# Padding tiles in SBUF so that a matmul's two operands start at chosen offsets, with a one-tile first load and a reordered tail, in a hybrid retention and SSD layer

## The chip, the cores and the metric

The kernel runs on one core of a Trainium2 chip. The core has a matrix engine (PE, with a queue PEld for weight loads), a vector engine (DVE), an activation engine (ACT), a general engine (POOL) and a queue that issues DMAs (SP). Each takes its instructions in order. Time is device microseconds of one execution, the median of three runs.

## What is computed

One layer over 16 learned meta tokens and 512 frames (L = 528) with a model width of 1024, all in float32:

```python
hn = _rmsnorm(h, norm1_w[i])
proj = (hn @ w_in[i]) * valid[None, :, None]
q, k, v, g, z, xbc, dt_raw = _split_cols(proj)
y_ret = _retention(q, k, v, g, pos, ret_norm_w[i])
y_ssd = _ssd(z, xbc, dt_raw, valid, conv_w[i], conv_b[i], dt_bias[i], a_log[i],
             d_skip[i], ssd_norm_w[i])
h = h + jnp.concatenate([y_ret, y_ssd], axis=-1) @ w_out[i]
u = _rmsnorm(h, norm2_w[i]) @ w_ff1[i]
h = h + jnp.square(jax.nn.relu(u)) @ w_ff2[i]
return _rmsnorm(h, final_norm_w)[:, CHUNK:]
```

`_retention` has 8 heads with decay over chunks of 64 frames and rotary q and k. `_ssd` (Mamba-2) has 4 groups of 4 heads: `x`, `B` and `C` go through a causal convolution of width 4 and silu, the step size `dt` through softplus, the chunks through a scan, and the result is gated by silu(z) and normalised.

## The kernel before, in words

Every large product is done with three matmuls on the fast float32 form: each operand is split into a high part (ACT, line 164) and a low part (DVE, line 165, source minus high part), and high x high, high x low and low x high are summed in PSUM (lines 342 to 344, `mm_k`). The normalised input stands transposed in SBUF as `hnh` and `hnl`, [128, 8 K tiles, 576] each, of which 528 columns are used. In `mm_cols` the weights (`wh`, two halves for high and low) are the stationary operand and a piece of the 528 columns is the moving one; 528 is more than the 512 columns of a PSUM bank, so each output tile is made in two pieces, `HV` = 272 and 256 columns, with 8 x 3 = 24 matmuls each. `C` leaves the first 12 columns out and has 260 and 256. In the `z` products (line 473) the columns of `hnh` and `hnl` are the stationary operand and the 256 weight columns move. FF1 (line 998) multiplies quarters of the weights with quarters `hs1` to `hs7` of the activations, 256 columns at a time (a Strassen-like scheme with 7 products); `wo` and FF2 have 512 columns and aren't touched.

Where in SBUF a tile starts follows from the pools: each tile is placed behind the last. `wh_tile` moves the start of a weight tile by 16 floats (64 bytes) per class `cls`, for which each tile is 128 floats longer than it needs to be:

```python
t = pool.tile([P, 8 * ZN], F32R, tag="w", name="wh")
return t[:, 16 * cls:16 * cls + 2048].rearrange("p (y n) -> p y n", y=2)
```

In time order the program has: the start (0 to 20 us: loads of the first weights `wzr` by ACT's queue and of the transposed input `xf` by SP's, `NWARM` matmuls on zeros that PE does meanwhile, the splits of both, the first `z` product), four SSD groups (20 to 187 us), eight retention heads (187 to 412), the output product (to 500), FF1 (to 672), FF2 with the tail (to 845).

An SSD group makes `B`, `C` and two `x` tiles: matmuls to a PSUM tile `pj`, DVE's eviction to `pre` (line 407), convolution in four DVE steps into `acc` (423, 425), silu on ACT into `bf`, `cf` or `xf` (427; this `xf` is not the input of the start). PE transposes those (`mtp`, `btp`, `xtp`), and ACT and DVE copy them out (`btm`, `bt`, `xmw`, `xdw`). In the first group PE sums the decays (`acs`, `acst`); ACT takes exponentials (`tea`, `cd`), which needs another activation table than silu, loaded by an ACT_TABLE_LOAD. `acst` goes through DRAM (`acsd`) and comes back as four broadcasts `lt`, to which DVE adds (509) and of which ACT takes the exponential (510). `zs` is silu(z) from PSUM (474), `mixs` copies the group's result (611).

The order in which the code is written isn't the order on the engines: the tile framework's scheduler orders instructions of each engine by its own estimates, inside what dependencies allow, except for instructions marked with `keep_in_program_order`.

At the end `fin_b(b)` adds the last half of token block b (1065, DVE), squares it (1067, ACT), `scale_b` of the block before follows (1083 on DVE, 1085 on ACT, with a DMA each), and POOL makes the block's 1/rms `rss`; the last block is done in two pieces of 256 columns.

Of the kernel before, what the change touches and what calls it, by code (L numbers as in the profile page):

```python
# [19 lines left out]
LP = 576  # L20
NWARM = 10
LAG = 2
# [53 lines left out]
def kernel(ctx, tc, x, meta, xtr, wzd, nfw, w_in, w_out, w1, w2, hrows, pcols, crope, cmask, cpack, cident, out, gpow):  # L76
# [66 lines left out]

    warm(NWARM)
    HV = ((0, 272), (272, 256))

# [3 lines left out]
    mt = startp.tile([M, D], F32, name="mt")  # L150
    for k in range(0, KT, 2):
        nc.scalar.dma_start(out=wzr[:, k:k + 2], in_=wzd[:, k:k + 2])
    for t0, n in HV:
        for k in range(0, KT, 2):
            o = KT + KT * t0 + k * n
            e = o + 2 * n
            if o == KT:
                o = 0
            nc.sync.dma_start(out=xf[:, o:e], in_=xtr[:, o:e])
# [46 lines left out]

    def u_z(w, c0, cls):

        loads = [(lambda r: r.rearrange("p (k c) -> p k c", c=256),
                  w[:, c0:c0 + 256].rearrange("(k p) c -> p k c", p=P))]  # L210
        return Unit(loads, lambda r, j: r[:, j * 1024:(j + 1) * 1024].rearrange("p (k c) -> p k c", c=256), 256, (cls, cls))

    class UnitZ0(Unit):
# [7 lines left out]

        def pair(self, k):

            j, k0 = divmod(k, 4)
            if k0 == 0:
                t = whl.tile([P, 8 * ZN], F32R, tag="w", name="wz").rearrange("p (y k c) -> p y k c", y=2, c=ZN)
                self.parts[j] = (t[:, 0], t[:, 1])
            hv, lv = self.parts[j]
            split(hv[:, k0:k0 + 2], lv[:, k0:k0 + 2], wzr[:, k:k + 2])

# [14 lines left out]
    for g in range(SG):  # L245
        add(("bc", g), u_cols(w_in, C_B + P * g, C_C + P * g))
        add(("x", g), u_cols(w_in, C_X + 256 * g, C_X + 256 * g + P, (1, 1)))
        if g:
            add(("z", g), u_z(w_in, C_Z + 256 * g, (g - 1) % 3))
    for h in range(RH):  # L250
        add(("qk", h), u_cols(w_in, C_Q + P * h, C_K + P * h, (1, 2)))
        add(("vg", h), u_cols(w_in, C_V + P * h, C_G + P * h, (3, 1)))
    for hf in range(2):
# [71 lines left out]
    nc.sync.dma_start(out=cst, in_=cpack)  # L325
    for k in range(0, KT, 2):
        if k:
            order[0].pair(k)
        for kk in (k, k + 1):
            gain_split(0, kk, ACT if k else DVE)  # L330
        if not k:
            order[0].pair(k)
    st["prep"] = 2
# [66 lines left out]
    def conv_silu(key, j, ct, tag, bufs, res, name, t_in=0, t_out=0, hook=None):  # L400
        wh, wl = part(key, j)
        pre = sw.tile([P, 3 + L], F32, tag="pre", name="pre")
        if t_in == 0:
            DVE.memset(pre[:, 0:3], 0.0)

        def evict(ps, t0, n):
            DVE.tensor_tensor(pre[:, 3 + t0:3 + t0 + n], ps[:, :n], rsr[:, t0:t0 + n], op=ALU.mult)

        out = []
        for t0, n in ((t_in, 272 - t_in), (272, 256)):  # L410
            ps = psum(pp, "pj")
            mm_cols(ps, n, wh, wl, t0)
            out.append((ps, t0, n))
            if not hook:
                evict(*out.pop())
        if hook:
            hook()
            for o in out:
                evict(*o)
        acc = sw.tile([P, L], F32, tag="acc", name="acc", bufs=1)  # L420
        cw = PC_CW + 4 * ct
        ts = slice(t_out, L)
        DVE.tensor_scalar(acc[:, ts], pre[:, t_out:L], pc[:, cw:cw + 1], None, op0=ALU.mult)
# [232 lines left out]
    def ret_proj(h, r):  # L656
# [10 lines left out]
        wh, wl = part(("qk", h), 1)  # L667
        for t0, n in HV:
            ps = psum(pp, "pk")
            mm_cols(ps, n, wh, wl, t0)  # L670
            rope_piece(kr, kt, ps, t0, n, t0)
# [3 lines left out]
        wh, wl = part(("vg", h), 0)  # L675
        for t0, n in HV:
            ps = psum(pp, "pv")
            mm_cols(ps, n, wh, wl, t0)
            ACT.activation(vf[:, t0:t0 + n], ps[:, :n], AF.Copy)
# [172 lines left out]

    def split_hs(q, pool, src):
        t = HS.get(q)
        if t is None:
            t = HS[q] = pool.tile([P, 2, 4, 256], F32R, name=f"hs{q}")
        split(t[:, 0].rearrange("p k n -> p (k n)"), t[:, 1].rearrange("p k n -> p (k n)"), src)

    def tok_gen(b):
# [4 lines left out]
        for j in range(2):  # L864
# [6 lines left out]
            if b == 1:  # L871
                split_hs(1 + j, None, R[j][0])
            yield
# [6 lines left out]
        while "t" not in FP:  # L880
            yield
        split_hs(6, FP["t"], t2)
        yield
        split_hs(5, FP["t"], R[0][0])
        sub(R[0][1], R[1][1], R[0][1])
        yield
        split_hs(7, FP["t"], R[0][1])
        yield
        sub(R[1][0], R[1][0], t2)
        split_hs(4, FP["t"], R[1][0])  # L890
        yield
        split_hs(3, FP["t"], R[1][1])

# [49 lines left out]
    def w1_prep(n, pool=None):  # L943
        if n >= len(seq) or n in wsp:
# [3 lines left out]
               5: lambda: s1s[g], 6: lambda: quarter(g, 0, 0), 7: lambda: quarter(g, 1, 0)}[q]()  # L948
        t = wh_tile(pool or whl, 1)
        split(t[:, 0, :], t[:, 1, :], src)  # L950
# [127 lines left out]
    def scale_b(b):  # L1078
        o = out[b * P:(b + 1) * P, :]
        w = 256 if b == NB - 1 else 512  # L1080
        for c in range(0, 512, w):
            l, r = slice(c, c + w), slice(512 + c, 512 + c + w)
            DVE.scalar_tensor_tensor(yo[b][:, r], xt[b][:, r], rss[b], nwb[:, r], op0=ALU.mult, op1=ALU.mult)
            nc.sync.dma_start(out=o[:, r], in_=yo[b][:, r])
            ACT.activation(yo[b][:, l], yo[b][:, l], AF.Copy, scale=rss[b])
            nc.scalar.dma_start(out=o[:, l], in_=yo[b][:, l])
# [66 lines left out]
```

## Time and profile before

| | us |
|---|---|
| median of 3 runs | 845.76 |
| lowest, highest | 845.34, 850.91 |
| profiled execution, of which span | 847.17, 845.4 |
| PE busy | 832.1 |
| DVE busy | 556.5 |
| ACT busy | 411.2 |

The profile is one execution; its span runs from the first to the last instruction, and 1.8 us lie around it. Busy time counts an engine's instructions, and matmuls overlap each other: a matmul of 256 columns is listed with 0.28 us although the next one starts after less than half of that. PE's granted clock was 0.998 of full speed in the mean.

### The profile page before, as it was taken

What the parts mean: (1) busy time and instruction counts of PE and PEld (TensorE: products, weight loads), DVE (VectorE), ACT (ScalarE), POOL (GpSimd) and SP (SyncE); (2) the same over time, 40 slices, a digit from 0 to 9 for tenths busy, and PEclk for the clock granted to TensorE, in tenths of its full rate; (3) what the DMA queues carried; (4) which work ended last, traced back from release to release, by engine and by line L of the source; (5) the groups of instructions that cost most, each with busy time, mean ns of one, the idle gap of its engine ahead of it and who ended that gap; (6) DMA issues with size and microseconds to landing.
All of it is one profiled execution on the core that took longest, in us unless ns stands there. A gap on an engine that the chain in (4) does not pass through costs nothing.

```text
span 845.4 us, 13366 instructions
## 1 busy us (share of the span) xinstructions
PE 832.1 (98%) x5556; PEld 759.2 (90%) x5556; DVE 556.5 (66%) x874; ACT 411.2 (49%) x693; POOL 29.8 (4%) x62
## 2 busy tenths in 40 slices
PE   8999999999999999999999999999999999999996
PEld 7999999999889999999888889999999888888884
DVE  6788997968745554556365539988887554474442
ACT  7755737272422233232453548577667643354432
POOL 1000000010000000000000000000000000010001
PEclk9999999999999999999999999999999999999999
DMA  9751333332331313131213213333334523332002
GB/s 316 252 178 50 100 101 100 95 106 76 101 100 50 100 51 100 51 101 50 100 53 102 96 50 100 101 100 101 100 101 137 188 100 99 100 100 100 0 1 100
DMA packets 85373, 84.70 MB, mean 100 GB/s; under 512 B 2464, under 2 KB 67744, under 8 KB 85312
## 3 DMA queue, kind: packets, MB, share of 16 engines
q1 hardware_dynamic: 84016, 81.68, 30.7%
q10 hardware_dynamic: 1296, 2.16, 0.7%
q8 instruction: 43, 0.70, 0.3%
q14 instruction: 18, 0.15, 0.1%
HBM read 81.71 MB, written 2.13 MB: 99 GB/s over the span
## 4 chain that ended last, share of the span: by engine, by line
PE 90%; DVE 3%; ACT 3%; DMA 2%; issue 2%; POOL 0%; POOLq 0%; ACTq 0%; SPq 0%
PE acc L781 10%; PE acc L782 10%; PE acc L780 10%; PE fb L998 7%; PE fd L998 5%; PE fa L998 4%; PE pz L473 3%; PE pj L344 3%; PE pj L342 3%; PE pj L343 3%; PE pv L344 2%; PE pv L343 2%; PE pv L342 2%; PE pk L342 2%; PE pk L344 2%; PE pk L343 2%
## 5 line engine op out<-in xcount | busy, mean ns | idle before, releaser
L164 ACT ACTIVATE wh<-wr 128x1024 fp32r<-128x1024 f32 x146 | 153.8, 1057 | 207.2 <-issue 81.6
L165 DVE TENSOR_TENSOR wh<-wr,wh 128x1024 fp32r<-128x1024 f32 x146 | 177.8, 1219 | 107.4 <-ACT wh L164 107.2
L781 PE MATMUL acc<-wh,mh 128*128 128x512 f32 x370 | 144.1, 390 | 0.5 <-DVE mh L165 0.5
L780 PE MATMUL acc<-wh,mh 128*128 128x512 f32 x370 | 144.2, 391 | 0.0
L782 PE MATMUL acc<-wh,mh 128*128 128x512 f32 x370 | 144.1, 389 | 0.0
L781 PEld LDWEIGHTS acc<-wh,mh 128*128 128x128 f32 x370 | 69.5, 188 | 15.0 <-DVE mh L165 0.9
L782 PEld LDWEIGHTS acc<-wh,mh 128*128 128x128 f32 x370 | 69.5, 188 | 14.6
L780 PEld LDWEIGHTS acc<-wh,mh 128*128 128x128 f32 x370 | 69.4, 188 | 14.0
L342 PE MATMUL pj<-hnh,wh 128*128 128x256 f32 (+2 forms) x256 | 73.7, 288 | 0.0
L343 PE MATMUL pj<-hnl,wh 128*128 128x256 f32 (+2 forms) x256 | 73.2, 286 | 0.0
L344 PE MATMUL pj<-hnh,wh 128*128 128x256 f32 (+2 forms) x256 | 72.5, 283 | 0.0
L998 PE MATMUL fb<-hs,wh 128*128 128x256 f32 x576 | 68.4, 277 | 0.4 <-DVE wh L165 0.4
L998 PEld LDWEIGHTS fb<-hs,wh 128*128 128x128 f32 x576 | 66.8, 188 | 0.7 <-DVE wh L165 0.6
L343 PEld LDWEIGHTS pj<-hnl,wh 128*128 128x128 f32 x256 | 48.5, 189 | 0.1
L342 PEld LDWEIGHTS pj<-hnh,wh 128*128 128x128 f32 x256 | 48.4, 189 | 0.0
L344 PEld LDWEIGHTS pj<-hnh,wh 128*128 128x128 f32 x256 | 48.4, 189 | 0.0
L998 PE MATMUL fa<-hs,wh 128*128 128x256 f32 x384 | 46.3, 277 | 0.3 <-ACT a_lo L1003 0.3
L998 PE MATMUL fd<-hs,wh 128*128 128x256 f32 x384 | 45.2, 277 | 0.0
L998 PEld LDWEIGHTS fa<-hs,wh 128*128 128x128 f32 x384 | 44.7, 188 | 0.5 <-ACT a_lo L1003 0.5
L998 PEld LDWEIGHTS fd<-hs,wh 128*128 128x128 f32 x384 | 44.5, 188 | 0.1
L164 ACT ACTIVATE mh<-a_lo 128x512 fp32r<-128x512 f32 x48 | 29.3, 621 | 19.2 <-PE acc L782 17.1
L165 DVE TENSOR_TENSOR mh<-a_lo,mh 128x512 fp32r<-128x512 f32 x48 | 32.5, 687 | 7.7 <-ACT mh L164 7.6
(270 smaller groups left out, 1646.6 us busy)
## 6 DMA issues: line engine op xcount, KB each, us to landing
wr<-in_w_ff_dram SPq DMA_DIRECT2D x30, 1024.0 KB, 5.3
wr<-in_w_in_dram SPq DMA_DIRECT2D x40, 512.0 KB, 4.8
wr<-in_w_out_dram SPq DMA_DIRECT2D x8, 1024.0 KB, 5.0
wr<-in_w_in_dram SPq DMA_DIRECT2D x7, 1024.0 KB, 8.1
lt<-acsd SPq DMA_DIRECT2D x16, 256.0 KB, 4.2
xt<-in_x_dram SPq DMA_DIRECT2D x4, 512.0 KB, 6.8
a_lo<-in_w_ff_dram SPq DMA_DIRECT2D x2, 1024.0 KB, 6.4
wzr<-in_wzd_dram ACTq DMA_DIRECT2D x4, 272.0 KB, 6.1
```

What stands on the lines that cost most here:

```text
L164: ACT.activation(dst_h, src, AF.Copy)
L165: DVE.tensor_tensor(dst_l, src, dst_h.bitcast(F32), op=ALU.subtract)
L342: PE.matmul(ps[:, :n], lhsT=wh[:, k, :], rhs=hnh[:, k, t0:t0 + n], start=(k == 0), stop=False)
L343: PE.matmul(ps[:, :n], lhsT=wh[:, k, :], rhs=hnl[:, k, t0:t0 + n], start=False, stop=False)
L344: PE.matmul(ps[:, :n], lhsT=wl[:, k, :], rhs=hnh[:, k, t0:t0 + n], start=False, stop=(k == KT - 1))
L473: PE.matmul(o, lhsT=a[:, k, tk], rhs=zp[k // 4][y][:, k % 4, :], start=(i == 0), stop=(i == len(seq) - 1))
L780: PE.matmul(acc[b], lhsT=s[:, 0, tk], rhs=wh[:, kk, :], start=(k == 0), stop=False)
L781: PE.matmul(acc[b], lhsT=s[:, 1, tk], rhs=wh[:, kk, :], start=False, stop=False)
L782: PE.matmul(acc[b], lhsT=s[:, 0, tk], rhs=wl[:, kk, :], start=False, stop=(k == nk - 1))
L998: PE.matmul(o, lhsT=w[:, y, k, cs], rhs=h[:, z, k, :], start=(q in (1, 6, 5) and t == 0 and k == 0 and i == 0), stop=(k == 3 and i == 2), ...
```

## The change

`hnh`, `hnl` and the `hs` tiles get pads of 64 bytes ahead (and of 192 behind), so that they start 64 bytes past a multiple of 256; all weight tiles that are stationary start at class 2 (128 bytes), and the moving weights of `z` at class 1 (64 bytes). The pieces of 528 columns are cut 256 and 272, in this order, where they were 272 and 256, so that the second piece starts at a multiple of 256 bytes behind the first; `C` has 244 and 272. With that the 256- and 272-column products have (moving, stationary) start at (64, 128) modulo 256 bytes, `z` of the first group aside. `hs3` to `hs7` are now allocated together. The first two loads of `wzr` and `xf` hold one K tile each, and their splits are done likewise; `NWARM` goes from 10 to 8. In `scale_b` the two scalings keep their place in program order, which puts the last block's sum ahead of the scaling of the block before.

```diff
-NWARM = 10
+NWARM = 8
...
+    hnp.tile([P, 16], F32, name="pad7")
     hnh, hnl = [hnp.tile([P, KT, LP], F32R, name=n)[:, :, :L] for n in ("hnh", "hnl")]
+    hnp.tile([P, 48], F32, name="pad8")
...
-    HV = ((0, 272), (272, 256))
+
+    HV, PV = ((0, 272), (272, 256)), ((0, 256), (256, 272))
...
-    for k in range(0, KT, 2):
-        nc.scalar.dma_start(out=wzr[:, k:k + 2], in_=wzd[:, k:k + 2])
+    KP = ((0, 1), (1, 2), (2, 4), (4, 6), (6, 8))
+    for k, e in KP:
+        nc.scalar.dma_start(out=wzr[:, k:e], in_=wzd[:, k:e])
     for t0, n in HV:
-        for k in range(0, KT, 2):
+        for k, e in KP if t0 == 0 else ((0, 2),) + KP[2:]:
             o = KT + KT * t0 + k * n
-            e = o + 2 * n
+            e = o + (e - k) * n
...
-        return Unit(loads, lambda r, j: r[:, j * 1024:(j + 1) * 1024].rearrange("p (k c) -> p k c", c=256), 256, (cls, cls))
+        return Unit(loads, lambda r, j: r[:, j * 1024:(j + 1) * 1024].rearrange("p (k c) -> p k c", c=256), 256, (1, 1))
...
-        add(("x", g), u_cols(w_in, C_X + 256 * g, C_X + 256 * g + P, (1, 1)))
+        add(("x", g), u_cols(w_in, C_X + 256 * g, C_X + 256 * g + P))
         if g:
-            add(("z", g), u_z(w_in, C_Z + 256 * g, (g - 1) % 3))
+            add(("z", g), u_z(w_in, C_Z + 256 * g))
     for h in range(RH):
-        add(("qk", h), u_cols(w_in, C_Q + P * h, C_K + P * h, (1, 2)))
-        add(("vg", h), u_cols(w_in, C_V + P * h, C_G + P * h, (3, 1)))
+        add(("qk", h), u_cols(w_in, C_Q + P * h, C_K + P * h))
+        add(("vg", h), u_cols(w_in, C_V + P * h, C_G + P * h))
...
-        for t0, n in ((t_in, 272 - t_in), (272, 256)):
+        for t0, n in ((t_in, 256 - t_in), (256, 272)):
...
-        for t0, n in HV:
+        for t0, n in PV:
             ps = psum(pp, "pk")
...
+    hs12.tile([P, 16], F32, name="pad3")
     HS = {q: hs12.tile([P, 2, 4, 256], F32R, name=f"hs{q}") for q in (1, 2)}
+    hs12.tile([P, 48], F32, name="pad4")
...
-        t = wh_tile(pool or whl, 1)
+        t = wh_tile(pool or whl, 2)
...
-            DVE.scalar_tensor_tensor(yo[b][:, r], xt[b][:, r], rss[b], nwb[:, r], op0=ALU.mult, op1=ALU.mult)
+            tc.keep_in_program_order(
+                DVE.scalar_tensor_tensor(yo[b][:, r], xt[b][:, r], rss[b], nwb[:, r], op0=ALU.mult, op1=ALU.mult))
             nc.sync.dma_start(out=o[:, r], in_=yo[b][:, r])
-            ACT.activation(yo[b][:, l], yo[b][:, l], AF.Copy, scale=rss[b])
+            tc.keep_in_program_order(ACT.activation(yo[b][:, l], yo[b][:, l], AF.Copy, scale=rss[b]))
             nc.scalar.dma_start(out=o[:, l], in_=yo[b][:, l])
```

The lines of the file move by 4 to 9. The scheduler orders the SSD groups otherwise, too, on all engines. Three places of it follow; `x3` behind a row is a count, and numbers behind a name tell buffers apart.

ACT in the first SSD group before, from the convolutions of `C` and the first `x` tile on:

```order
L164 ACTIVATE wh<-wr 128x1024
L427 ACTIVATE cf<-acc,pc 128x512
L378 ACTIVATE acst<-acs 16x512
L427 ACTIVATE xf<-acc,pc 128x528
L392 ACT_TABLE_LOAD
L392 ACTIVATE tea<-tna 128x80
L391 ACTIVATE dt_436<-dt_436 128x80
L393 ACTIVATE cd<-acst 128x80
L527 ACTIVATE bt<-btp 128x384
```

and after:

```order
L168 ACTIVATE wh<-wr 128x1024
L432 ACTIVATE cf<-acc,pc 128x512
L168 ACTIVATE wh<-wr 128x1024
L383 ACTIVATE acst<-acs 16x512
L397 ACT_TABLE_LOAD
L397 ACTIVATE tea<-tna 128x80
L432 ACT_TABLE_LOAD
L432 ACTIVATE xf<-acc,pc 128x528
L396 ACT_TABLE_LOAD
L396 ACTIVATE dt_440<-dt_440 128x80
L398 ACTIVATE cd<-acst 128x80
L532 ACTIVATE bt<-btp 128x384
```

`xf` of the first `x` tile stood between `acst` and the table load of the exponentials; now a split is ahead of `acst`, `tea` with its table load is ahead of `xf`, and silu's table is loaded again.

DVE in the first SSD group before, around the second `x` tile (`pre` of 256 columns is its first row):

```order
L407 TENSOR_TENSOR pre<-pj,rsr 128x256
L423 TENSOR_SCALAR acc<-pre,pc 128x528
L425 SCALAR_TENSOR_TENSOR acc<-pre,pc,acc 128x528
L165 TENSOR_TENSOR wh<-wr,wh 128x1024
L425 SCALAR_TENSOR_TENSOR acc<-pre,pc,acc 128x528
L407 TENSOR_TENSOR pre<-pj,rsr 128x272
L425 SCALAR_TENSOR_TENSOR acc<-pre,pc,acc 128x528
L509 TENSOR_SCALAR lt<-lt,tna 128x128 x5
L407 TENSOR_TENSOR pre<-pj,rsr 128x256
L509 TENSOR_SCALAR lt<-lt,tna 128x128 x5
```

and after:

```order
L412 TENSOR_TENSOR pre<-pj,rsr 128x256
L514 TENSOR_SCALAR lt<-lt,tna 128x128 x3
L412 TENSOR_TENSOR pre<-pj,rsr 128x272
L514 TENSOR_SCALAR lt<-lt,tna 128x128
L428 TENSOR_SCALAR acc<-pre,pc 128x528
L399 TENSOR_TENSOR tdw<-tdt,dt_440 128x80
L430 SCALAR_TENSOR_TENSOR acc<-pre,pc,acc 128x528
L514 TENSOR_SCALAR lt<-lt,tna 128x128
L430 SCALAR_TENSOR_TENSOR acc<-pre,pc,acc 128x528
L514 TENSOR_SCALAR lt<-lt,tna 128x128
L430 SCALAR_TENSOR_TENSOR acc<-pre,pc,acc 128x528
L514 TENSOR_SCALAR lt<-lt,tna 128x128
```

The additions to `lt`, which wait for its DMA, stood behind the tile's convolution and now stand ahead of the eviction of its second piece and between the steps.

ACT in the second SSD group before, around the silu of its second `x` tile (`xf`) and of the first three of its four `z` pieces (`zs`):

```order
L474 ACTIVATE zs<-pz,rsc 128x256
L427 ACTIVATE xf<-acc,pc 128x528
L474 ACTIVATE zs<-pz,rsc 128x256
L510 ACT_TABLE_LOAD
L510 ACTIVATE lt<-lt 128x512
L474 ACT_TABLE_LOAD
L474 ACTIVATE zs<-pz,rsc 128x256
L523 ACTIVATE btm<-mtp 16x128
```

and after:

```order
L479 ACTIVATE zs<-pz,rsc 128x256
L616 ACTIVATE mixs<-ytp,pc 128x512
L432 ACTIVATE xf<-acc,pc 128x528
L515 ACT_TABLE_LOAD
L515 ACTIVATE lt<-lt 128x512
L479 ACT_TABLE_LOAD
L479 ACTIVATE zs<-pz,rsc 128x256
L616 ACTIVATE mixs<-ytp,pc 128x512
L479 ACTIVATE zs<-pz,rsc 128x256
```

Before, two `zs` follow each other with one `xf` between; now the second `zs` stands behind `xf`, a load, `lt` and another load, and half of the `mixs` copies stands behind it.

## Rows read from the trace of the kernel before

**Rows 1.** The page's part 1, and the weight splits' subtractions on DVE (part 5).

```profile
PE 832.1 (98%) x5556; PEld 759.2 (90%) x5556; DVE 556.5 (66%) x874; ACT 411.2 (49%) x693; POOL 29.8 (4%) x62
...
L165 DVE TENSOR_TENSOR wh<-wr,wh 128x1024 fp32r<-128x1024 f32 x146 | 177.8, 1219 | 107.4 <-ACT wh L164 107.2
```

**Rows 2.** Whom PE waited for: line, releaser, us in total, times, longest.

```profile
PE st L553 <- ACT btm L523: 0.7, 1, 0.7
```

**Rows 3.** Timeline of PE: start, us, instruction; first and last counted row of pieces.

```profile
38.55 0.29 PE L342 MATMUL pj<-hnh,wh 128*128 128x272 f32 x1
...
41.40 0.29 PE L344 MATMUL pj<-hnh,wh 128*128 128x272 f32 x1
...
43.90 0.28 PE L343 MATMUL pj<-hnl,wh 128*128 128x256 f32 x1
...
46.53 0.28 PE L344 MATMUL pj<-hnh,wh 128*128 128x256 f32 x1
...
253.00 0.29 PE L344 MATMUL pk<-hnh,wh 128*128 128x272 f32 x1
...
255.66 0.29 PE L344 MATMUL pk<-hnh,wh 128*128 128x272 f32 x1
255.79 0.28 PE L342 MATMUL pk<-hnh,wh 128*128 128x256 f32 x1
...
258.39 0.28 PE L344 MATMUL pk<-hnh,wh 128*128 128x256 f32 x1
...
561.28 2.09 PE L998 MATMUL fa<-hs,wh 128*128 128x256 f32 x17
```

**Rows 4.** Timeline of ACT at the start.

```profile
2.92 1.28 ACT L164 ACT_TABLE_LOAD   x1 [2.92 <-issue]
5.35 0.66 ACT L164 ACTIVATE wz<-wzr 128x544 fp32r<-128x544 f32 x1 [1.15 <-DMA wzr<-in_wzd_dram]
```

**Rows 5.** Timeline of PE and DVE at the end.

```profile
835.73 1.52 PE L807 MATMUL acc<-wh,mh 128*128 128x512 f32 x6
...
837.87 0.75 DVE L1083 SCALAR_TENSOR_TENSOR yo<-xt,rss,nwb 128x512 f32<-128x512 f32 x1 [1.69 <-POOL rss L1074]
838.54 0.87 DVE L1065 SCALAR_TENSOR_TENSOR xt<-acc,rs,xt 128x256 f32<-128x256 f32 x2
```

**Rows 6.** Timeline of ACT, DVE and PE in the first SSD group.

```profile
38.80 1.06 ACT L164 ACTIVATE wh<-wr 128x1024 fp32r<-128x1024 f32 x1 [2.77 <-issue]
39.08 0.74 DVE L425 SCALAR_TENSOR_TENSOR acc<-pre,pc,acc 128x512 f32<-128x512 f32 x1
...
39.89 0.43 DVE L407 TENSOR_TENSOR pre<-pj,rsr 128x272 f32<-128x272 f32 x1
40.24 0.23 DVE L368 SCALAR_TENSOR_TENSOR dtv<-dtv,dt 128x80 f32<-128x80 f32 x1
...
42.73 0.59 ACT L378 ACTIVATE acst<-acs 16x512 f32<-16x512 f32 x1 [2.15 <-PE acs L377]
...
44.80 0.74 ACT L427 ACTIVATE xf<-acc,pc 128x528 f32<-128x528 f32 x1 [1.48 <-DVE acc L425]
...
45.55 1.28 ACT L392 ACT_TABLE_LOAD   x1
...
46.65 0.27 PE L519 MATMUL mtp<-idt,xf 128*16 128x128 f32 x1
```

**Rows 7.** Timeline of DVE, first addition to `lt`.

```profile
53.87 1.07 DVE L509 TENSOR_SCALAR lt<-lt,tna 128x128 f32<-128x128 f32 x5 [1.81 <-DMA lt<-acsd]
```

**Rows 8.** Tile `lt`: time from issue to landing of its DMAs.

```profile
DMA to landing us min/median/max: 3.2/4.2/7.4
```

**Rows 9.** Timeline of ACT and PE's weight loads in the fourth SSD group.

```profile
178.51 0.74 ACT L427 ACTIVATE xf<-acc,pc 128x528 f32<-128x528 f32 x1 [1.69 <-DVE acc L425]
...
182.51 0.47 ACT L474 ACTIVATE zs<-pz,rsc 128x256 f32<-128x256 f32 x1
...
183.98 0.19 PEld L473 LDWEIGHTS pz<-wh,hnh 128*128 128x128 f32 x1 [0.22 <-ACT zs L474]
```

More of the change, by code (lines that the diff above doesn't have):

```diff
@@ L205, in u_cols, with u_z @@
         return Unit(loads, views, P, cls)
-    def u_z(w, c0, cls):
+    def u_z(w, c0):
         loads = [(lambda r: r.rearrange("p (k c) -> p k c", c=256),
                   w[:, c0:c0 + 256].rearrange("(k p) c -> p k c", p=P))]
-        return Unit(loads, lambda r, j: r[:, j * 1024:(j + 1) * 1024].rearrange("p (k c) -> p k c", c=256), 256, (cls, cls))
+        return Unit(loads, lambda r, j: r[:, j * 1024:(j + 1) * 1024].rearrange("p (k c) -> p k c", c=256), 256, (1, 1))
     class UnitZ0(Unit):
@@ L220, in load, with tiles @@
             pass
-        def pair(self, k):
+        def tiles(self, k, e):
             j, k0 = divmod(k, 4)
@@ L228, in pair @@
             hv, lv = self.parts[j]
-            split(hv[:, k0:k0 + 2], lv[:, k0:k0 + 2], wzr[:, k:k + 2])
+            e0 = k0 + e - k
+            split(hv[:, k0:e0], lv[:, k0:e0], wzr[:, k:e])
     def u_rows(w, k0, c0):
@@ L325 @@
     nc.sync.dma_start(out=cst, in_=cpack)
[L326 to L332, printed above, removed]
+    for k, e in KP:
+        if k > 1:
+            order[0].tiles(k, e)
+        for kk in range(k, e):
+            gain_split(0, kk, ACT if k > 1 else DVE)
+        if k < 2:
+            order[0].tiles(k, e)
     st["prep"] = 2
@@ L675, in ret_proj @@
         wh, wl = part(("vg", h), 0)
-        for t0, n in HV:
+        for t0, n in PV:
             ps = psum(pp, "pv")
@@ L851, with split_hs @@
     FP = {}
[L853 to L856, printed above, removed]
+    def split_hs(q, src):
+        t = HS[q]
         split(t[:, 0].rearrange("p k n -> p (k n)"), t[:, 1].rearrange("p k n -> p (k n)"), src)
@@ L871, in tok_gen @@
             if b == 1:
-                split_hs(1 + j, None, R[j][0])
+                split_hs(1 + j, R[j][0])
             yield
@@ L881, in tok_gen @@
             yield
-        split_hs(6, FP["t"], t2)
+        split_hs(6, t2)
         yield
-        split_hs(5, FP["t"], R[0][0])
+        split_hs(5, R[0][0])
         sub(R[0][1], R[1][1], R[0][1])
         yield
-        split_hs(7, FP["t"], R[0][1])
+        split_hs(7, R[0][1])
         yield
         sub(R[1][0], R[1][0], t2)
-        split_hs(4, FP["t"], R[1][0])
+        split_hs(4, R[1][0])
         yield
-        split_hs(3, FP["t"], R[1][1])
+        split_hs(3, R[1][1])
     def fin1(b, acc):
@@ L1039, in first_products @@
                 FP["t"] = tc.alloc_tile_pool(name="hst", bufs=1, side="right", reuse_waits="tile")
+                FP["t"].tile([P, 16], F32, name="pad5")
+                HS.update({q: FP["t"].tile([P, 2, 4, 256], F32R, name=f"hs{q}") for q in (6, 5, 7, 4, 3)})
+                FP["t"].tile([P, 48], F32, name="pad6")
             if n == at[(6, 0)]:
```

## The prediction

> **What bounds the kernel now.** I read the page first. PE is busy 98% of the span, DVE 66%, ACT 49% [rows 1]; so time is won by matmuls that follow each other faster, by a shorter start or end, or by removing the few waits of PE. Next I read what PE waits for: the longest single wait after the start is 0.7 us, for ACT's copy of `btm` in the first SSD group [rows 2]. There is thus little to win from waits and much room to lose: an engine that is off the chain today needs to fall behind by a microsecond only once to show in the end. Third, I read the start-to-start time of matmuls of one size at different places of the program, since a matmul's listed length (0.28 us) overlaps the next one.
>
> **Part 1, the addresses.** In the built program the tiles start at multiples of 64 bytes; I write (moving, stationary) for the two operands' first bytes modulo 256. The pitch is the start of a later row minus that of an earlier one, divided by the number of matmuls between [rows 3]:
> 256 columns at (64,128), retention `pk`: (258.39 - 255.79)/23 = 113.0 ns. 256 columns at (64,64), the second `x` tile: (46.53 - 43.90)/22 = 119.5 ns. 256 columns at (0,64), FF1: (2.09 - 0.28)/16 = 113.1 ns. 272 columns at (0,128), `pk`: (255.66 - 253.00)/21 = 126.7 ns. 272 columns at (0,64), `x`: (41.40 - 38.55)/23 = 123.9 ns.
> What is quick in these rows is the stationary operand 64 bytes past the moving one, (0,64) and (64,128); a difference of 0 or 128 costs 5 to 6% at 256 columns and 2% at 272. The change puts all of these at (64,128). For 256 columns that case has its row, 113.0. For 272 it has none: between 113.0 x 272/256 = 120.1 (if only the columns counted) and 126.7 (no better than now); I take 123.9, the row with the same difference.
> The sum: `x`, 192 matmuls of 256 columns from 119.5 to 113.0, 1.25 us; `pv`, 192 of 256 columns at (64,192), priced like `x`, 1.25; `z` of groups 1 to 3, of whose 288 matmuls two thirds have a difference that isn't 64, another 192 x 6.5 ns = 1.25; 272 columns of `pk`, `pv` and `B`, 480 x 2.8 ns = 1.34. `x`'s own 272-column pieces gain nothing (123.9 already), `C` has 516 columns in two pieces before and after, the 1344 matmuls of FF1 run at 113 already, and the 512-column products keep their difference. Total **-5.1 us**. The ends come from the 768 pieces of 272 columns: 3.8 ns less each gives -8.0, 2.8 ns more gives -2.9.
> The Trainium skill's page "TensorE: Matmul & The Clock Gate", section "Back-to-back issue gap", gives N/2.4 + 2.5 ns for a single stream, whatever the operands' addresses: an estimate of 109 ns at 256 columns and 116 at 272. The trace lies 4 to 11 ns above it and differs by address, so it doesn't bear this out; if the rule held, this part would be worth nothing (the third rival).
>
> **Part 2, the start.** ACT issues five pieces of `wzr` in place of four. In the built program the fifth issue waits for the landing of the first piece, because eight DMA semaphores are used in turn, and behind it on ACT's queue stand the table load and the first weight split. Before, the load ran at 2.92 to 4.20, beside the transfer, and the split at 5.35 when `wzr` had landed [rows 4]. Now a piece of half the size may land some 0.6 us earlier (half of the 1.15 that ACT waited after the load), the load (1.28) follows it, and the first split starts near 6.0 (5.9 to 6.6) instead of 5.35. The pieces behind it land when they did before. So of this at most 0.5 to 1.3 us reach PE, and most of it is caught up, because PE waits for the second pair's landing anyway. Fewer warm matmuls end PE's warm stretch two matmuls earlier. I take **+0.4 us**, ends -0.1 (the smaller first piece wins after all) and +1.4 (nothing is caught up).
>
> **Part 3, the end.** PE's last matmul ends at 837.25. DVE then first waits for POOL's `rss` of block 2, scales it at 837.87, and starts the last block's sum at 838.54 [rows 5]. In the new order the sum stands first and can start about 837.4, so 1.1 us earlier; behind it come ACT's squares, POOL, the last scale and the output DMAs. Block 2's scale then falls into POOL's time; its own DMA issue (0.37 us on ACT) may hold the last scale by 0.1. **-1.0 us**, ends -0.7 and -1.2.
>
> **Part 4, what the reorder moves along.** With the pieces of `x`, `B`, `C` swapped, the scheduler writes other orders on ACT, DVE and SP all through the SSD groups. No row of before shows these orders; I bound each place from the rows of the work that now stands in the queue.
> First group, ACT: `xf` of the first `x` tile stood ahead of a table load and now stands behind two, one for `tea`'s exp and one back to silu; a third follows it. DVE, which finished the convolution of `C` at 39.82 before, now has in front of that: a weight split's subtraction (1.2), an eviction (0.35 to the next start) and four short steps (0.15 each by the same count), 2.1 us in all, so it is done near 41.9 [rows 1, 6]. From there ACT does `cf` and `xf`, 0.74 each, a split 1.06, `acst` 0.59, two loads of 1.28 and the small `tea`, some 0.2: 5.9 us, less some 0.1 of overlap at each of four places: 47.4. PE stood at the transposes of that tile at 46.65 without a wait; the same matmuls are ahead of them now and save about 0.3. Wait **+1.1** (0 to 2.7).
> Second place in that group: DVE's additions to `lt`, which waited 1.81 us for the broadcast DMA [rows 7] at a point where little depended on them, now stand in front of the eviction and the convolution of the second `x` tile. The DMA needs 3.2 to 7.4 us to land after its issue [rows 8]; with 3.2, since no weight load stands ahead of it any more, the convolution (some 3.7 us with the `lt` steps between) ends 0.5 to 1 us after PE needs it, and `btm`, for which PE waited 0.7, comes behind more `lt` steps: **+1.5** (0 to 3.0).
> Second group: ACT now has, after the second `x` tile's `xf`: load, `lt`, load, `zs`, half of `mixs`, `zs`. The `z` pieces use PSUM banks that only `zs` frees, so PE's fourth piece stands behind that queue. The fourth group has this very order before already: from `xf` at 178.51 to `zs` at 182.51 it took 4.0 us, and PE waited only 0.22 for it [rows 9], because it had a `z` piece of 24 matmuls (2.7 to 2.9 us by the pitches above) and eleven transposes to do. In the new order seven of those eleven stand ahead of the fourth piece, an estimated 0.1 us less for each that is gone: a wait of 0.6 if `xf` ends with PE's piece. In the second group DVE's convolution stands behind `lt` as well, which may hold `xf` by up to 2.4: 3.0 in all. **+1.3** over before, nearer to the fourth group's row. Groups three and four, without that delay: **+0.4** each (0 to 1.2).
> Total 1.1 + 1.5 + 1.3 + 0.8 = **+4.7 us**, ends 0 and +11.
> The Trainium skill's "ScalarE: Activation LUTs", section "What ACT_TABLE_LOAD costs", puts a set switch at 2.66 us, 1.28 load and 1.38 drain. The trace shows no drain: the fourth group's 4.0 us [rows 9] hold `xf` 0.74, two loads of 1.28 and `lt`, some 0.6. By that section's figure the first place alone would be an estimated 2.8 us worse.
>
> **Sum.** -5.1 + 0.4 - 1.0 + 4.7 = -1.0 us on the profiled execution's 847.17 (span 845.4). That run lies 1.4 above the median of 845.76; taken from the median, the forecast is **844.8 us**.
>
> **Rivals.**
> (a) The new orders cost nothing: DVE and ACT are 66% and 49% busy [rows 1], and before's longest wait stays below 0.7 us, and in the fourth group the same order of ACT costs 0.22 [rows 2, 9]. Against it: at the first two places PE has no slack. Then -5.1 + 0.4 - 1.0 = -5.7: 840.1, with 272 columns at 120.1 ns 837.2.
> (b) Slower: ACT's order around `zs` is paid in full in each of the groups two to four. If the fourth `z` piece waits 3.0 us in each, with 2.6 from the first group, the waits sum to 11.6, and the kernel takes 845.76 + 11.6 - 5.1 + 0.4 - 1.0 = 851.7. It decides where DVE's convolution ends more than about 1 us after PE's second `z` piece in all three groups. For it: `xf` in the fourth group waited 1.69 us for DVE already [rows 9]. Against: the fourth group's row, 0.22.
> (c) The pitch doesn't follow the addresses, but what runs beside the matmuls; then the change doesn't do what it says, and 0.4 - 1.0 + 4.7 = +4.1 remains: 849.9. Against it: the pitches are constant over whole pieces of 24 matmuls, in stretches with quite different work on the other engines.
>
> **Chances.** Forecast 0.55, (a) 0.27, (b) 0.12, (c) 0.06. The range that leaves out 2 in 10 goes from 838.5 (most of (a)) to 852.5 ((b)'s value with most of the start's bound). A measurement of this kernel tells about 1% from no change, 8.5 us: below 837.3 only with (a) and 120.1 ns together, 0.07; above 854.2 only with (b) and the late start, 0.06; the rest, 0.87.
>
> **What would show it.** Part 1: the pitch of `pv`'s and `x`'s 256-column pieces falls to 113 ns, and that of the 272-column pieces says which bound held. Part 2: the first weight split at 5.9 to 6.6. Part 3: the last block's sum right behind PE's end. Part 4: waits of PE on ACT's `xf`, `btm` and `zs` near 42 to 100 us, of 1 to 3 us each. The prediction is wrong if those waits stay below 1 us in all (then (a)), or if the products of the retention heads, whose order hardly changes, don't get faster (then (c)).

## The result and the profile after

The changed kernel takes 856.13 us in the median of 20 runs (850.20 to 858.48), before 848.33 in as many (845.29 to 851.63). The ratio is 1.0081, with a 95% interval of 1.006 to 1.0102: slower by about 7 us. The forecast was 844.8, the range 838.5 to 852.5. Both kernels have executions that are about 5 us longer than their others (of before's 20, ten took 845.3 to 846.3 us and ten 850.3 to 851.6), from a stretch of FF1 that the last section shows, so that a median also depends on how many of them there were; the two profiles compared here have none of it (847.17 before, 852.28 after).

The page of the changed kernel:

```profile
span 850.5 us, 13363 instructions
PE 832.0 (98%) x5554; PEld 759.7 (89%) x5554; DVE 557.9 (66%) x875; ACT 408.1 (48%) x692; POOL 28.3 (3%) x62
```

PE's busy time is the same as in [rows 1], but the span is 5.1 us longer. By the first matmuls of each stage, PE is 0.8 us late at the first `pj` (20.76, before 19.94), 7.7 at the first `pq` of the heads (194.78, before 187.06), 5.6 at the output product (417.66, before 412.05), still 5.6 at the end of FF1, and 5.9 at PE's last matmul (843.11, before 837.25); the span ends 5.1 late. So the start loses 0.8, the SSD groups lose 6.9, the heads win 2.1, FF2 loses 0.2, and the end behind PE wins 0.7.

What PE waited for (line, releaser, us in total, times, longest):

```profile
PE pz L478 <- ACT zs L479: 4.4, 3, 2.8
PE mtp L524 <- ACT xf L432: 2.1, 1, 2.1
...
PE xtp L545 <- ACT cd L398: 0.2, 1, 0.2
PE st L558 <- ACT btm L528: 0.2, 1, 0.2
```

In place of one wait of 0.7 for `btm` [rows 2] stand three for `zs`, 4.4 in sum, and one of 2.1 for `xf`. The windows behind the two longest, which ended at 49.66 and 98.53 (busy us of each engine, the column ahead of the last two is PE's granted clock):

```profile
50.00:54.00 4.00, 3.83 (x22) 3.53 (x21) 3.22 (x10) 3.63 (x7) 0.00 (x0) 0.57 0.95 311
54.00:58.00 4.00, 4.00 (x35) 3.96 (x35) 4.00 (x15) 3.57 (x4) 0.00 (x0) 1.00 0.04 14
98.00:102.00 4.00, 3.47 (x17) 3.47 (x18) 0.00 (x0) 3.96 (x8) 0.00 (x0) 0.57 0.00 0
102.00:106.00 4.00, 4.00 (x37) 4.00 (x36) 2.57 (x5) 3.65 (x4) 0.00 (x0) 1.00 0.01 4
```

In the first of the two windows behind each wait the clock is at 0.57 in the mean, and in the second at full. With a lower level of 0.5 (1.2 GHz) that is 2 x (1 - 0.57) x 4 = 3.4 us at the lower level, half of which, 1.7 us, is lost: 3.4 us for the two, beside the waits themselves. The matmuls show it. PE's timeline across the first wait:

```profile
47.23 0.28 PE L349 MATMUL pj<-hnh,wh 128*128 128x272 f32 x1
49.66 0.28 PE L524 MATMUL mtp<-idt,xf 128*16 128x128 f32 x1 [2.14 <-ACT xf L432]
...
52.71 0.41 PE L348 MATMUL pj<-hnl,wh 128*128 128x256 f32 x1
52.92 0.41 PE L349 MATMUL pj<-hnh,wh 128*128 128x256 f32 x1
53.14 0.41 PE L347 MATMUL pj<-hnh,wh 128*128 128x256 f32 x1
```

Three 256-column matmuls of the second group's `B` tile, which PE does next, start 0.21 us apart (52.71, 52.92, 53.14), where the pitch is 0.113 at the full clock.

ACT's timeline in the first group shows the queue that the prediction named:

```profile
43.83 0.73 ACT L432 ACTIVATE cf<-acc,pc 128x512 f32<-128x512 f32 x1 [7.65 <-DVE acc L430]
...
46.00 1.28 ACT L397 ACT_TABLE_LOAD   x1
47.29 0.27 ACT L397 ACTIVATE tea<-tna 128x80 f32<-128x80 f32 x1
47.58 1.28 ACT L432 ACT_TABLE_LOAD   x1
48.87 0.73 ACT L432 ACTIVATE xf<-acc,pc 128x528 f32<-128x528 f32 x1
```

`cf` starts at 43.83, when DVE is done with the convolution of `C` (43.79; I had put it at 41.9), and `xf` 5.0 us behind it, after two table loads. PE was at the transposes at 47.5. In the second group:

```profile
93.07 0.74 ACT L432 ACTIVATE xf<-acc,pc 128x528 f32<-128x528 f32 x1 [3.45 <-DVE acc L430]
93.82 1.28 ACT L515 ACT_TABLE_LOAD   x1
95.12 0.63 ACT L515 ACTIVATE lt<-lt 128x512 f32<-128x512 f32 x1
95.76 1.28 ACT L479 ACT_TABLE_LOAD   x1
97.06 0.47 ACT L479 ACTIVATE zs<-pz,rsc 128x256 f32<-128x256 f32 x1
97.43 0.68 ACT L616 ACTIVATE mixs<-ytp,pc 128x512 f32<-128x512 f32 x1
98.00 0.47 ACT L479 ACTIVATE zs<-pz,rsc 128x256 f32<-128x256 f32 x1
```

`xf`, load, `lt`, load, `zs`, `mixs`, `zs`: 5.4 us in a row, as in the fourth group before [rows 9], but begun late, since DVE's convolution held `xf` until 93.07.

The heads, where the order hardly changed, show the addresses (PE's timeline; `pk` 256, `pk` 272, `pv` 256):

```profile
260.18 0.28 PE L348 MATMUL pk<-hnl,wh 128*128 128x256 f32 x1
...
262.68 0.28 PE L349 MATMUL pk<-hnh,wh 128*128 128x256 f32 x1
...
262.91 0.29 PE L348 MATMUL pk<-hnl,wh 128*128 128x272 f32 x1
...
265.63 0.29 PE L349 MATMUL pk<-hnh,wh 128*128 128x272 f32 x1
...
267.66 0.28 PE L348 MATMUL pv<-hnl,wh 128*128 128x256 f32 x1
...
270.40 0.29 PE L348 MATMUL pv<-hnl,wh 128*128 128x272 f32 x1
```

256 columns of `pk`: (262.68 - 260.18)/22 = 113.6 ns; 272 columns: (265.63 - 262.91)/22 = 123.6, before 126.7 [rows 3]; `pv`, 24 matmuls from 267.66 to 270.40: 114.2.

In the SSD groups the gain is only partly there. Two `z` pieces of the third group, one after the other on PE, whose operands both start at (64,128) (moving, stationary; the pieces lie 512 bytes apart in `hnh` and `hnl`):

```profile
134.52 0.28 PE L478 MATMUL pz<-wh,hnh 128*128 128x256 f32 x1
...
137.22 0.28 PE L478 MATMUL pz<-wh,hnh 128*128 128x256 f32 x1
...
138.29 0.28 PE L478 MATMUL pz<-wh,hnl 128*128 128x256 f32 x1
...
140.79 0.28 PE L478 MATMUL pz<-wh,hnh 128*128 128x256 f32 x1
```

The first has (137.22 - 134.52)/23 = 117.4 ns, the second (140.79 - 138.29)/22 = 113.6, at full clock both. Of the twelve `z` pieces in this profile seven run near 113 and four near 118 (the one left over is at the lower clock), and of the eight 256-column pieces of `x` six near 114 and two near 118.

The start, on ACT and on PE:

```profile
3.93 1.28 ACT L168 ACT_TABLE_LOAD   x1 [3.93 <-DMA wzr<-in_wzd_dram]
5.22 0.75 ACT L168 ACTIVATE wz<-wzr 128x272 fp32r<-128x272 f32 x2
7.79 0.66 ACT L168 ACTIVATE wz<-wzr 128x544 fp32r<-128x544 f32 x1 [1.82 <-DMA wzr<-in_wzd_dram]
```

```profile
6.78 1.11 PE L451 MATMUL pz<-wz,hnh 128*128 128x272 f32 x4
```

The first split is at 5.22, earlier than 5.35 [rows 4], not later; the small first piece landed by 3.93. But the second pair landed for a split at 7.79, where the corresponding one had been at 6.84, and PE ran its first matmuls at what their pitch shows to be the lower clock: four of them in 1.11 us, where before four took 0.76 with a wait in front.

The end, on DVE and ACT:

```profile
843.15 0.88 DVE L1073 SCALAR_TENSOR_TENSOR xt<-acc,rs,xt 128x256 f32<-128x256 f32 x2 [1.31 <-PE acc L812]
...
845.67 0.51 ACT L1094 ACTIVATE yo<-yo,rss 128x256 f32<-128x256 f32 x1 [0.48 <-POOL rss L1082]
...
846.61 0.51 ACT L1094 ACTIVATE yo<-yo,rss 128x256 f32<-128x256 f32 x1 [0.43 <-ACT yo L1094]
```

The last block's sum starts at 843.15, right at PE's end (843.11). Before, 1.3 us lay between the two (837.25 and 838.54). Of the 1.2 us that this brings, 0.4 is lost at the second of the two last scales on ACT: 846.61, behind the DMA issue of the first.

### The profile page after: what moved, and what is told of

The parts are those of the page before. It is cut to its first block, busy times and chain, and to the rows that moved or that the text cites. A ratio compares the mean times of both kernels' runs of the same rounds, so it can differ in the third digit from the quotient of the medians.

```text
span 850.5 us, 13363 instructions
## 1 busy us (share of the span) xinstructions
PE 832.0 (98%) x5554; PEld 759.7 (89%) x5554; DVE 557.9 (66%) x875; ACT 408.1 (48%) x692; POOL 28.3 (3%) x62
## 4 chain that ended last, share of the span: by engine, by line
PE 87%; DVE 7%; ACT 3%; DMA 1%; issue 1%; POOL 1%; POOLq 0%; ACTq 0%; DVEq 0%
PE acc L785 10%; PE acc L787 10%; PE acc L786 10%; PE fb L1003 7%; PE fd L1003 5%; PE fa L1003 4%; PE pj L347 2%; PE pj L348 2%; PE pj L349 2%; PE pv L347 2%; PE pk L348 2%; PE pv L348 2%; PE pv L349 2%; PE pk L347 2%; PE pk L349 2%; PE pq L347 2%
## 5 line engine op out<-in xcount | busy, mean ns | idle before, releaser
L347 PE MATMUL pj<-hnh,wh 128*128 128x272 f32 (+2 forms) x256 | 73.9, 289 | 0.0
L348 PE MATMUL pj<-hnl,wh 128*128 128x272 f32 (+2 forms) x256 | 73.2, 286 | 0.0
L349 PE MATMUL pj<-hnh,wh 128*128 128x272 f32 (+2 forms) x256 | 73.1, 285 | 0.0
L478 PE MATMUL pz<-wh,hnh 128*128 128x256 f32 x192 | 37.5, 290 | 4.4 <-ACT zs L479 4.4
```

Source lines behind the costliest of these rows:

```text
L347: PE.matmul(ps[:, :n], lhsT=wh[:, k, :], rhs=hnh[:, k, t0:t0 + n], start=(k == 0), stop=False)
L348: PE.matmul(ps[:, :n], lhsT=wh[:, k, :], rhs=hnl[:, k, t0:t0 + n], start=False, stop=False)
L349: PE.matmul(ps[:, :n], lhsT=wl[:, k, :], rhs=hnh[:, k, t0:t0 + n], start=False, stop=(k == KT - 1))
L478: PE.matmul(o, lhsT=a[:, k, tk], rhs=zp[k // 4][y][:, k % 4, :], start=(i == 0), stop=(i == len(seq) - 1))
```

## The experiments

All ratios are to the kernel before, with their 95% intervals.

**e1, the new order alone.** The kernel before with the SSD pieces swapped:

```diff
-        for t0, n in ((t_in, 272 - t_in), (272, 256)):
+        for t0, n in ((t_in, 256 - t_in), (256, 272)):
```

> The kernel before with one edit: the pieces of x, B and C in the SSD groups are cut 256 and 272 in place of 272 and 256; no pads, no new classes, old start and tail. Its engines get the changed kernel's orders in the SSD groups. Theory 1 (the new orders cost the time: PE waits for xf, zs and the exponentials, and runs at half clock after the two longest waits): waits of about 2.1 us at the first transposes and 2.8 us at the fourth z piece of the second group, half clock after both, +8 to +10 us against before, ratio 1.009 to 1.012. Rival (the addresses or the pads cost the time): no difference beyond 1 us, ratio 0.999 to 1.001.

Ratio 1.0099 (1.0078 to 1.012). Its waits of PE:

```profile
PE pz L473 <- ACT zs L474: 3.8, 3, 2.8
PE mtp L519 <- ACT xf L427: 2.2, 1, 2.2
PE st L553 <- ACT btm L523: 1.2, 1, 1.2
```

One edited line, with no pad and no class, brings the waits of the changed kernel and its loss. From 38 us to the end of the SSD groups ACT, DVE and PE have the changed kernel's orders. The rival (addresses or pads) is out as the cause of the loss: the swap does move the start of the second piece (in `x` from (64,64) to (0,64), the quicker of the two in [rows 3]; in `B` and `C` the other way), but by the pitches of the pieces that is well under 1 us. The half clock came once, behind the wait for `zs` (99 to 103 us: 0.57), not twice as expected.

**e2, the old SSD pieces in the changed kernel**, e1's edit the other way round.

> The changed kernel with one edit undone: the SSD pieces are 272 and 256 again, so that the SSD groups have before's orders on all engines; pads, classes, retention pieces, start and tail stay new. Theory 1: -1.2 (z) -1.2 (pv) -1.1 (272 columns of pk and pv) +0.9 (start) -0.6 (tail) and about +1 for B and C whose 256-column pieces now start at (128,128): about -2 us against before, ratio 0.996 to 0.999; no wait of PE above 1 us in the SSD groups. Rival (addresses or pads): +6 us as in the changed kernel, ratio 1.006 to 1.009.

Ratio 0.9994 (0.9977 to 1.0011), profiled span 844.5; the longest wait in the SSD groups is 0.6 us (`ytp` for DVE's `y`). With e1 this puts the loss of the SSD groups on the order that follows from the swap: from the first `pj` to the first `pq` they take 165.7 us here, 174.0 in the changed kernel. The span would be shorter but for the start: PE's first `z` product kept the pitch of the lower clock until 13.9 us in this profile, and the first `pj` came at 23.08, 3.1 us later than before.

**e3, ten warm matmuls in the changed kernel.**

```diff
-NWARM = 8
+NWARM = 10
```

> The changed kernel with 10 warm matmuls in place of 8. If the first z product runs at half clock because PE was idle for 1.1 us after the earlier end of the warm matmuls, it now runs at full clock from its first matmul at about 5.7 us, and the whole is 1 to 1.5 us shorter than the changed kernel (about +4 against before's profiled execution, ratio 1.005 to 1.007). If the five loads and the late table load cost it, nothing changes against the changed kernel.

Ratio 1.0089 (1.006 to 1.0117): no gain that can be told, although PE's first product now ran at full clock (four matmuls in 0.66 us). It reached the third K tile sooner and waited there 1.2 us for ACT's `hnh`; the first `pj` came at 20.46, 0.3 earlier. So the clock was not what held the start in the changed kernel's profile; in e2's, where the lower pitch lasted until 13.9 us, PE was another 2.3 us later.

**e4, old pieces, ten warm matmuls, and the weights of `x`, `B`, `C` at 192 bytes**, so that their 256-column pieces, at 128 bytes now, have the difference of 64:

```diff
-        add(("bc", g), u_cols(w_in, C_B + P * g, C_C + P * g))
-        add(("x", g), u_cols(w_in, C_X + 256 * g, C_X + 256 * g + P))
+        add(("bc", g), u_cols(w_in, C_B + P * g, C_C + P * g, (3, 3)))
+        add(("x", g), u_cols(w_in, C_X + 256 * g, C_X + 256 * g + P, (3, 3)))
```

> The changed kernel with 272 and 256 in the SSD groups, 10 warm matmuls, and the weights of x, B and C at 192 bytes, so that their 256-column pieces start at (128,192) and their 272-column pieces at (64,192). Theory 1: -1.2 (z) -1.2 (pv) -1.1 (pk, pv) -1.2 (x, 256) +0.5 (x, 272) -0.6 (tail) -0.4 (start): about -5 us, ratio 0.993 to 0.996. Rival (addresses or pads cost the time): +5 us.

Ratio 0.9984 (0.9963 to 1.0004), profiled span 841.6 against 845.4: less than the expected 0.993 to 0.996, and the interval touches 1. In the profile the heads win 2.1 us; the SSD groups take 165.8, as e2's do.

**e5, a PSUM tile for each `z` piece** in the changed kernel:

```diff
-            ps = psum(pp, "pz")
             for cc in range(2):
+                ps = psum(pp, "pz")
```

> The changed kernel with a PSUM tile for each z piece in place of one for two pieces. If the 2.8 us before the fourth z piece of the second group (and 0.8 in groups three and four) come from the write after read on the shared tile, behind zs on ACT's queue, they vanish, and with them any half clock that follows: 4 to 6 us less than the changed kernel, ratio to before 1.001 to 1.004. If ACT's queue holds PE anyway (the ring of four tiles, the copies behind it), the wait moves to the next user and the ratio stays at 1.007 or above.

Ratio 1.0133 (1.0097 to 1.0169): slower than before; against the changed kernel (1.006 to 1.0102) the two intervals just meet. It is the second expectation that held, the wait moving to the next user. Its waits:

```profile
PE yd L595 <- DVE lt L579: 4.1, 10, 1.7
```

The waits for `zs` are gone, so the shared tile was what held PE there. But the exponentials of `lt` came later with the new order, and PE now waits 4.1 us for `lt` at `yd`. The SSD groups take 175.7 us, 1.7 more than in the changed kernel; another 1.7 of this profile's 9.1 more are the start's (first `pj` at 22.45), and 4.9 are FF1's longer pitch.

**e6, PE kept busy in the first wait:**

```diff
         psm = psum(pm, "mtp")
+        for _ in range(14 if g == 0 else 0):
+            PE.transpose(psm[:, 384:512], ident, ident)
```

> The changed kernel with 14 transposes of the identity into an unused part of the PSUM tile, ahead of the first group's transposes, where PE waits 2.1 us; they take some 1.5 us of that wait. If the half clock after the wait (50.5 to 54 us in the changed kernel's profile) follows from PE having been idle, the clock stays at full speed there and this stretch is about 1.6 us shorter; the wait itself, which ACT ends, doesn't get longer. Rival: the clock falls for another reason, and stays half there.

Ratio 1.0066 (1.0037 to 1.0096). The windows (PE's busy us first, granted clock third from the end):

```profile
50.00:54.00 4.00, 2.93 (x24) 2.70 (x25) 1.56 (x7) 2.01 (x5) 0.00 (x0) 1.00 0.83 242
54.00:62.00 8.00, 5.84 (x37) 5.61 (x36) 8.00 (x23) 6.89 (x10) 0.00 (x0) 0.79 0.29 93
```

With 1.7 us of transposes in it, the wait for `xf` was down to 0.8 and the clock stayed at full from 50 to 54. But the scheduler moved the second tile's transposes ahead, where PE now waited 2.2 us for `xf`, and there the clock fell (0.79 in the mean of 54 to 62). So here the lower clock came with the wait for `xf`, wherever that was; the total says nothing of its price, since the wait only moved.

**e7, the addresses and the tail with the old start**: e4 with the four loads of before.

> The pads and classes, 272 and 256 in the SSD groups with their weights at 192 bytes, 256 and 272 in the heads, the new tail, but the start of before (four loads, 10 warm matmuls). Theory 1: -4.5 from the addresses, -0.6 from the tail, nothing from the start: about -5 us against before, ratio 0.993 to 0.995, and 0.5 less than with the new start. Rival (addresses worth nothing): ratio 0.999.

Ratio 0.9959 (0.9936 to 0.9981), profiled span 841.5. A little less than expected, which the interval includes: the addresses and the tail are worth 3.9 us between the profiles. The heads win 2.1 of it and the end 0.6. ACT, DVE and PE have before's orders in the SSD groups, so pads and classes alone don't change them, and these groups take 166.2 us: 1.0 less than in before's profile, but no less than in e9's and e10's (165.9 and 165.7), which have before's addresses there.

**e8, e7 with e5's edit.**

> The kernel of e7 with a PSUM tile for each z piece. Before's waits of PE for zs (0.2 to 0.4 in each of three groups) go: another 0.5 to 1 us less than e7, ratio 0.992 to 0.994. Rival: the scheduler's other order that comes with it costs more than that, ratio above e7's.

Ratio 0.9927 (0.9903 to 0.9951), 841.6 us in the median, the best of all and faster than both kernels. The profile is 1.7 us shorter than e7's (839.7), though the two intervals overlap. It has no wait of PE for `zs`, and none above 0.2 for `lt`, where e5 had 4.1. The scheduler's order differs from e7's on all engines here, so how much of the gain is the tile's own is not shown.

**e9, the tail alone** (the new `scale_b` in the kernel before).

> The kernel before with the new scale_b alone (scalings kept in program order, so that the last block's sum goes ahead of the scaling of the block before). By the prediction's part 3 the last output comes 1.0 us earlier; the changed kernel's profile says 0.7 (7.4 us from PE's end to the end of the span, where it was 8.15). Ratio 0.9988 to 0.9992. Rival: the output DMAs set the end, ratio 1.000.

Ratio 0.9982 (0.9957 to 1.0007); from PE's end to the end of the span 7.45 us, before 8.10. The gain of 0.7 is in the trace, too small for the interval.

**e10, the start alone** (first loads of one K tile, 8 warm matmuls, in the kernel before).

> The kernel before with the new start alone: first loads of one K tile, 8 warm matmuls. By the changed kernel's profile the first pj matmul comes 0.8 us later than before (20.76 against 19.94), so +0.8 us, ratio 1.0005 to 1.0015. By the prediction's part 2 +0.4.

Ratio 1.0016 (0.9992 to 1.004): if anything a loss, of the expected size.

**e11, ACT's order repaired in the changed kernel** by two orderings without a wait. `NOSYNC` is the kind of dependency that orders two instructions on one engine without a semaphore; `x0_i` is the recorded silu of the first `x` tile, `zs_i` that of the third `z` piece's `zs`:

```diff
-        ACT.activation(tea, tna, AF.Exp, scale=-1.0)
+        i = ACT.activation(tea, tna, AF.Exp, scale=-1.0)
+        tc.add_manual_dep(i.ins, r0["x0_i"].ins.name, NOSYNC, reason="behind xf")
...
-            ACT.activation(pl[h], pl[h], AF.Exp)
+            i = ACT.activation(pl[h], pl[h], AF.Exp)
+            if g:
+                tc.add_manual_dep(i.ins, r["zs_i"].ins.name, NOSYNC, reason="behind zs")
```

> The changed kernel with its pieces, addresses, start and tail, and two orderings added on ACT without a wait: tea's exponential stays behind the silu of the first x tile, and each group's exponentials of lt stay behind the zs of the third z piece, with the table loads that go with them. Theory 1 (ACT's order with the table loads between is what PE waits for): the wait for xf falls from 2.1 to about 0.7 us, those for zs from 2.8, 0.8 and 0.8 to 0.3 each, no half clock after them; 6 to 8 us less than the changed kernel, ratio to before 0.997 to 1.001. Rival (DVE's order, with lt ahead of the convolutions, holds everything anyway): less than 2 us gained, ratio above 1.005.

Ratio 1.0011 (0.9988 to 1.0034), 847.78 in the median: by the ratios 6 of the 7 us come back. By the profiles it is less: the SSD groups take 170.9 us, 174.0 in the changed kernel, 166.2 in e7. A few instructions of DVE and PE move with ACT's. Waits of PE:

```profile
PE mtp L531 <- ACT xf L434: 3.3, 2, 2.5
...
PE xtp L552 <- ACT cd L400: 1.2, 1, 1.2
```

The waits for `zs` are gone, and the first one for `xf` is 0.8. In this profile one of 2.5 for the second `xf` of the first group comes in its place (DVE, then ACT):

```profile
54.84 0.29 DVE L518 TENSOR_SCALAR lt<-lt,tna 128x128 f32<-128x128 f32 x1 [2.16 <-DMA lt<-acsd]
```

```profile
57.59 0.73 ACT L434 ACTIVATE xf<-acc,pc 128x528 f32<-128x528 f32 x1 [3.35 <-DVE acc L432]
```

DVE's addition to `lt` at 54.84 had waited 2.2 us for the broadcast DMA, the convolution's steps stand between and behind such additions, and `xf` came at 57.59. Behind that wait the clock was at 0.57 from 58 to 62 us.

**e12, e11 with the old start.**

> The kernel of e11 with the start of before (four loads, 10 warm matmuls). Theory 1: 0.8 us less than e11, ratio 0.995 to 0.999; if all of the addresses' 5 us come through, at or below e7's 0.996.

Ratio 0.9986 (0.9964 to 1.0008). Its waits:

```profile
PE xtp L552 <- ACT cd L400: 1.2, 1, 1.2
...
PE mtp L531 <- ACT xf L434: 0.5, 1, 0.5
```

```profile
46.00:50.00 4.00, 2.32 (x15) 1.97 (x15) 2.19 (x6) 3.76 (x7) 0.00 (x0) 0.89 0.69 206
50.00:54.00 4.00, 4.00 (x25) 4.00 (x25) 4.00 (x12) 2.08 (x3) 0.00 (x0) 0.68 0.60 196
```

The SSD groups take 168.9 us, 2.7 more than e7's. PE waits 1.2 us in the first group for `cd`, which with ACT's other exponentials stands behind `xf` now, and although this wait is short, the clock fell right behind it (0.89 and 0.68 in these windows, which is 2 x (0.11 + 0.32) x 4 = 3.4 us at the lower level and 1.7 lost, as above): together about what is missing. By their profiles e7 (841.5) and e8 (839.7), whose SSD pieces are the old ones, remain better than this kernel (844.0).

## Why the prediction was wrong, point by point

**Part 1, the addresses: right in the heads, too large in the SSD groups.** The sum was -5.1 with 113.0 and 123.9 ns; in the heads the changed kernel runs at 113.6 and 123.6, and where 2.3 was due, they won 2.1. Rival (c) is refuted for them: `pv` has the new pitch in the profiles of the kernels with the new addresses, and the old one, 120.0 (2.76 us for 23 matmuls), in e9's and e10's. In the SSD groups 2.8 was due (`x` and `z`, 1.25 each, and the part of `B`). By the pitches of their pieces I estimate 1.4, since several pieces of `x` and `z` run near 118 ns at the very offsets that were priced at 113. With before's orders even less of it arrived: e4 and e7 need as long for these groups as e9 and e10. In e7 PE's waits there (gaps above 0.1 us) sum to 1.8 us, in e9 to 0.8.

**Part 2, the start: size near, mechanism wrong.** Forecast +0.4, measured +0.8 at the first `pj`. I expected the table load to delay the first split; the first piece landed early enough for it. The loss came at the second pair, which landed a microsecond later, so that the first tiles' head start was lost there, at either clock (e3). The bound of +1.4 was too small: with the new start and 8 warm matmuls the first `pj` comes at 20.7 to 23.1 us in six profiles, with the old start at 19.4 to 19.9 in six.

**Part 3, the tail: right in kind, -0.7 for -1.0.** I had the DMA issue between the two last scales at 0.1; it cost 0.4.

**Part 4, the waits: here the prediction failed.** Its step "Total 1.1 + 1.5 + 1.3 + 0.8 = +4.7 us" had the mechanism and was mis-sized, and it left out what the waits do to the clock. The SSD groups lost 6.9 net against before's profile, and 8.1 and 8.4 against e9's and e10's, which have before's SSD groups.
The first place cost 2.1, not 1.1: DVE was done with `C` 1.9 us later than I counted, 0.8 of it the start's delay. At the second place, which I put at 1.5, PE waited 0.2 in the changed kernel's profile; e11 shows that the same place can cost 2.5 where the broadcast lands late. The second group cost 2.8 where I took 1.3, "nearer to the fourth group's row": ACT's queue was that of the fourth group, but `xf` came late behind DVE, which was the upper end (3.0). Groups three and four cost 0.8 each, not 0.4. These waits make 2.1 + 0.2 + 2.8 + 1.6 = 6.7 us. The missing term is the 3.4 us lost at the lower clock after the two longest waits: with it 10.1, less the 0.7 for `btm` [rows 2] and 0.6 for `ytp` that PE waited in before's profile, 8.8. With the 1.4 of faster streaming taken off, 7.4 is left, within the 6.9 to 8.4 that were lost. The clock stood neither in the sum nor in rival (b), which had the mechanism and ended at 851.7.
By e1 and e2 the whole loss comes with the new order. Restoring part of ACT's order brings back 3.1 us of the SSD groups' time in e11's profile and 5.1 in e12's, of some 8. So ACT's order has a large part in it; how much is DVE's own wasn't separated. The drain that the Trainium skill's "ScalarE: Activation LUTs" ("What ACT_TABLE_LOAD costs") adds to each load isn't the reason: in the second group `xf` to `zs` took 97.06 - 93.07 = 3.99 us, and `xf`, two loads and `lt` alone make 0.74 + 2.56 + 0.63 = 3.93.

## What to carry to other kernels

A change of the pieces' order or sizes passes through the scheduler, while pads and classes alone left the orders as they were (e7): compare the orders of all engines, and look for every table load and every DMA wait that has moved ahead of something that PE needs. Price a wait of PE with the lower clock that may stand behind it, not by its length alone: here that cost 1.7 us where it came, behind waits of 1.2 (e12), 2.1 and 2.8 us, and it didn't come behind every one. And try each edit of a bundle by itself: here the pads, the classes and the new tail with the old piece order and start win 0.4%, and 0.7% with a PSUM tile more, while one line that swaps two pieces loses 1%.

## What the runs showed of the hardware

FF1 has two pitches. In before's profile 885 matmuls fall into 100 us of it, 113.0 ns each; in e9's, a kernel with the same FF1 and the same addresses there, 852, which is 117.4 (windows, PE's busy us with its count first):

```profile
546.00:646.00 100.00, 100.00 (x885) 100.00 (x884) 86.36 (x93) 71.34 (x97) 2.55 (x4) 1.00 0.34 106
```

```profile
546.00:646.00 100.00, 100.00 (x852) 100.00 (x851) 82.81 (x89) 68.03 (x91) 2.45 (x4) 1.00 0.33 101
```

Both have full clock and a PE that is never idle. In e9's profile FF1 is 5.0 us longer (147.5 us from the first to the last `fd`, before 142.4). From its first `fa` to the end of its last `fd` it takes 163.5 us in eleven of the fourteen profiles and 168.4 in three: e5's, e9's and e11's, two of them with the new addresses. That is the difference of 5 us between executions of one kernel. Inside one execution, too, pieces with the same offsets run at either pitch, as the two `z` pieces of the changed kernel show. So the offsets alone don't set the pitch; what chooses between the two stays open.

The lower clock did not follow every long wait: in e6 a wait of 2.4 us for `zs` was followed by full clock, in e3 one of 2.7 (1.00 from 97 to 105), and in e1 the one of 2.2 for `xf` (granted clock 1.00 from 45 to 62 and from 60 to 75, the wait ending at 48.77). Yet it followed one of 1.2 in e12. What tells these apart stays open, too.
